# A decoder block on one core: the splits of the routing stage moved from GpSimd to VectorE, an f32 gate matrix, and a deeper run-ahead with activations in DRAM

## Chip, cores and metric

The kernel runs on one core of a Trainium2 chip. The metric is the device time of one execution, in microseconds.

## What is computed

One decoder block on 256 tokens of width 2048, all in float32: a mixer (retention and dilated attention), attention to 256 memory tokens, and the part that the change touches, a product-key expert layer. From the normed rows `hf` a query product gives scores against two sets of 128 keys per head (8 heads). Per token and head the best 16 of each set are taken, their 256 sums formed, the best 16 of these chosen, and a softmax over them gives 16 gates. Each choice names an expert (i1, i2) out of 128 × 128 = 16384. The result is

    a = gelu(hf @ u_tab[i].T);   y = sum over the 128 choices of (a * gate) * v_tab[i]

A last RMS norm follows.

## The kernel before

The expert layer is computed densely: all 16384 columns of the first table `u` are multiplied, in 32 chunks of 512, and all rows of the second table `v`; a gate matrix G (256 × 16384, mostly zeros) stands in for the choice. So the whole kernel is one stream of 464 weight pieces of 128 × 4 × 512 floats (1 MiB), and a piece is 24 TensorE matmuls of 512 columns: every f32 operand is split into two parts `hi` + `lo` (ScalarE writes `hi`, line 973; a subtraction writes `lo`, line 974), and three products make one exact product (lines 197 to 199).

*Order.* The program is written out by hand: each engine runs its instructions in the order in which the Python code emits them. `ahead` (line 966) emits the loads, on SP's queue, and the splits, two pieces ahead of the products (three raw buffers, so loads run about five pieces ahead). Between pieces `tick` (line 119) advances background generators. A generator that yields a cost may go on within a budget: 4.0 a tick, half of it when `fine` is set, and then there is a second tick in the middle of each piece. `fine` holds from the first piece of `u` until the gate matrix is done.

*Routing* (one generator, `route`): `route_top` (line 655, 32 steps of a top 16 over 128 keys), `route_pairs` (670, twice 8 heads of sums and a top 16 over 256, then one-hot selections of the key numbers, lines 701 to 704), `route_gates` (709: Exp on ScalarE, sums on VectorE, then on TensorE the transposes of line 726), and `gate_matrix` (741). All but these transposes, the Exp and some copies is VectorE's.

*Gate matrix.* In 32 steps of 8 tokens, VectorE builds, for each 4 tokens, bf16 one-hot rows for i2 (line 755) and i1 (756), and three products of the latter with the gate's three bf16 parts (758); TensorE sums 3 products per token (767, bf16, 128 columns); ScalarE copies them (768) and SP's queue writes 512 KB to G in DRAM (769). The matmuls of a step are emitted one step later than its one-hots.

*Tables.* 11 chunks of `u` (RUN_AHEAD) run before the first piece of `v`; their splits' `lo`, and those of the query product `w_pq`, are on GpSimd (`"pool"` in lines 935 and 942, taken up in 974). `evac_u` (777) writes a chunk's Gelu into an SBUF unit that is kept until `weigh` (787) loads the chunk's columns of G on SP's queue, multiplies (808) and transposes them (`to_T`, 168) for the second table. Then groups of 8 pieces of `v` alternate with 8 pieces of `u` until `u` is used up. The SBUF buffers called `unit` are a pool of 29.

Of the kernel before, what the change touches and what calls it, by code (L numbers as in the profile page):

```python
# [31 lines left out]
RUN_AHEAD = 11  # L32
# [3 lines left out]
TICK = 4.0  # L36

# [33 lines left out]
def block_kernel(ctx, tc, a, out):  # L71
# [47 lines left out]
    def tick():  # L119
        """One step of each; a step that yields a cost lets the next follow within the budget."""  # L120
        for g in list(active):
            spent, most = 0.0, TICK * (0.5 if fine[0] else 1.0)
            try:
                while spent < most:
                    spent += next(g) or TICK
            except StopIteration:
                active.remove(g)

    def add(g):
        active.append(g)  # L130
        return g
# [9 lines left out]
    def piece(ap, fn, lo_eng=None):  # L141
        prog.append((ap, fn, lo_eng))

    def call(fn):
        prog.append((None, fn, None))

# [54 lines left out]
    def chunks(wap, lhs, nk, order, evac, lo_eng=None):  # L201
        """Row products: for chunk n, k group kq in `order`, acc[n] += lhs[kq].T @ w piece."""
# [20 lines left out]
        for n, kq in order:  # L223
            c = seen.get(n, 0)
            seen[n] = c + 1
            piece(wap[n * nk + kq], make(n, kq, c == 0, c == nk - 1), lo_eng)
# [28 lines left out]
    def make_trig():  # L255
        """cos, sin, -sin of f32(position) * angle, its multiple of 2 pi taken off exactly."""
# [54 lines left out]
    def evac_rot(kind, key):  # L311
        """Rotated rows from [4 heads x first halves | 4 heads x second halves]."""
# [342 lines left out]
    def route_top(n):  # L655
        """The 16 best keys of each half query of chunk n, both token blocks."""
        while sc_rows[n] is None:
            yield
        for tb in range(2):
# [5 lines left out]
            for i in range(4):  # L665
                top16(rt[tb]["v"][:, 4 * n + i], rt[tb]["i"][:, 4 * n + i], sc_rows[n][:, tb, i], work([128]))
                yield 1.0
        sc_rows[n] = 0

    def route_pairs(tb):  # L670
        """Top 16 of the 256 sums per head, their experts' two key numbers and gates."""
# [10 lines left out]
        for h0 in range(0, 8, 4):  # L682
            combo = unit([4, 256])
            for h in range(h0, h0 + 4):
# [4 lines left out]
                yield 2.0  # L689
# [19 lines left out]
    def route_gates():  # L709
# [12 lines left out]
        for tb in range(2):  # L722
# [4 lines left out]
            rest = uc[:, 3]  # L727
            tt = uc[:, 4:6].rearrange("p a b -> p (a b)").bitcast(BF).rearrange("p (s t) -> p s t", t=128)
            i3 = uc[:, 0].bitcast(BF)[:, 0:128]
            nc.scalar.copy(rest, tp[:, 2])  # L730
            for s in range(2):
                nc.scalar.copy(tt[:, s], tp[:, s])
            nc.scalar.copy(tt[:, 2], rest)
            nc.vector.tensor_sub(rest, rest, tt[:, 2])
            nc.vector.tensor_copy(tt[:, 3], rest)
            nc.vector.tensor_sub(rest, rest, tt[:, 3])
            nc.vector.tensor_copy(i3, rest)
            rt[tb] = {"T": [tt[:, 0], tt[:, 1], tt[:, 2], tt[:, 3], i3]}
        yield

    def gate_matrix():
# [3 lines left out]
        iota4 = cp.tile([128, 128, 4], BF, name="iota4")  # L745
        nc.vector.tensor_copy(iota4, bc(iota[:, :, None], [128, 128, 4]))
        prev = None
        for tb, t0 in [(tb, t0) for tb in range(2) for t0 in range(0, 128, 8)] + [(None, None)]:
            cur = []
            if tb is not None:  # L750
                it = rt[tb]["T"]
                for t1 in (t0, t0 + 4):
                    oh = unit([4, 128, 4], BF)
                    col = [bc(z[:, None, t1:t1 + 4], [128, 128, 4]) for z in it]
                    nc.vector.tensor_tensor(oh[:, 0], iota4, col[1], op=OP.is_equal)  # L755
                    nc.vector.tensor_tensor(oh[:, 3], iota4, col[0], op=OP.is_equal)  # L756
                    for j in (1, 2, 3):
                        nc.vector.tensor_tensor(oh[:, j], oh[:, 3], col[1 + j], op=OP.mult)  # L758
                    cur.append(oh)
            if prev is not None:  # L760
                ptb, p0, ohs = prev
                gs = unit([8, 128])
                for j, oh in enumerate(ohs):
# [7 lines left out]
            yield  # L771
# [5 lines left out]
    def evac_u(c, acc):  # L777
# [3 lines left out]
        ga[c] = g  # L781
# [5 lines left out]
    def weigh():  # L787
        """Expert activations times gates, transposed for the second table's products."""
# [12 lines left out]
        for c in range(N_CH):  # L801
            while c not in ga or c > 2 * v_at[0] + 3:
# [4 lines left out]
            g, m = ga.pop(c), w.pop(c)  # L807
# [127 lines left out]
    chunks(a["w_pq"], hf_T, KQ, late, evac_rows_T(pq_T, "rstd2"), "pool")  # L935

    def u_chunk(c, eng=None):
        chunks(a["u"][c * KQ:c * KQ + KQ], hf_T, KQ, straight(0, 1), lambda _, acc: evac_u(c, acc), eng)

    call(lambda: fine.__setitem__(0, True))  # L940
    for c in range(RUN_AHEAD):
        u_chunk(c, "pool")
# [23 lines left out]
    def ahead(n):  # L966
        while at["split"] < min(n + SPLIT_AHEAD + 1, len(stream)):
# [33 lines left out]
    for ap, fn, _ in prog:  # L1001
# [29 lines left out]
def _pieces(w, cols=None):  # L1031
    """[K, N] -> [N/512 * K/512, 128, 4, 512]: blocks of 512 x 512, a k row per partition."""
# [66 lines left out]
```

## Time and profile before

| | us |
|---|---|
| median of 3 runs (lowest, highest) | 2840.21 (2840.13, 2842.31) |
| span of the profiled execution | 2843.3 |
| TensorE matmul busy | 2764.3 (97%) |
| VectorE busy | 1698.7 (60%) |
| ScalarE busy | 1160.1 (41%) |
| GpSimd busy | 378.0 (13%) |

The page gives the profiled execution's span, from the first to the last instruction, and no other time of its own. Matmuls overlap, so TensorE's busy share says only whether it had something to do; how fast it went is read from the spacing of starts. The page also cuts the span into 40 slices of 71 us, a digit for the tenths that an engine was busy.

### The profile page before, as it was taken

What the parts mean: (1) busy time and instruction counts of PE and PEld (TensorE: products, weight loads), DVE (VectorE), ACT (ScalarE), POOL (GpSimd) and SP (SyncE); (2) the same over time, 40 slices, a digit from 0 to 9 for tenths busy, and PEclk for the clock granted to TensorE, in tenths of its full rate; (3) what the DMA queues carried; (4) which work ended last, traced back from release to release, by engine and by line L of the source; (5) the groups of instructions that cost most, each with busy time, mean ns of one, the idle gap of its engine ahead of it and who ended that gap; (6) DMA issues with size and microseconds to landing.
All of it is one profiled execution on the core that took longest, in us unless ns stands there. A gap on an engine that the chain in (4) does not pass through costs nothing.

```text
span 2843.3 us, 31283 instructions
## 1 busy us (share of the span) xinstructions
PE 2764.3 (97%) x12898; PEld 2296.9 (81%) x12898; DVE 1698.7 (60%) x1872; ACT 1160.1 (41%) x1053; POOL 378.0 (13%) x153
## 2 busy tenths in 40 slices
PE   9999999999999999999299999999999999999998
PEld 7888888888888888888188788888888888888886
DVE  6565457785643445179999655455554555545664
ACT  6444334433554434444133334333343333433333
POOL 1111110011000000778133400000000000000001
PEclk9999999999999999999699999999999999999999
DMA  8554555576655445545156655555555555555653
GB/s 291 192 181 169 191 180 181 202 263 218 246 199 188 156 145 179 179 176 194 58 163 178 198 195 203 205 192 199 207 204 204 191 200 207 203 204 201 220 207 127
DMA packets 118736, 546.95 MB, mean 192 GB/s; under 512 B 10176, under 2 KB 42944, under 8 KB 59712
## 3 DMA queue, kind: packets, MB, share of 16 engines
q1 hardware_dynamic: 113488, 526.46, 53.3%
q0 software_dynamic: 5104, 18.48, 1.8%
q8 instruction: 101, 1.65, 0.2%
q14 instruction: 43, 0.35, 0.0%
HBM read 521.83 MB, written 23.07 MB: 192 GB/s over the span
## 4 chain that ended last, share of the span: by engine, by line
PE 84%; DVE 12%; issue 1%; POOL 1%; DMA 0%; ACT 0%; SPq 0%; POOLq 0%; DVEq 0%
PE acc L197 27%; PE acc L199 27%; PE acc L198 27%; DVE unit L758 3%; DVE unit L756 2%; PE tp L180 2%; DVE unit L703 1%; DVE unit L755 1%; DVE unit L685 1%; DVE unit L701 1%; POOL unit L327 1%; PE sm L610 0%; PE sm L579 0%; DVE unit L648 0%; DVE unit L645 0%
## 5 line engine op out<-in xcount | busy, mean ns | idle before, releaser
L197 PE MATMUL acc<-hi,unit 128*128 128x512 f32 x3712 | 1461.8, 394 | 6.9 <-ACT hi L993 6.9
L199 PE MATMUL acc<-hi,unit 128*128 128x512 f32 x3712 | 1448.1, 390 | 0.0
L198 PE MATMUL acc<-lo,unit 128*128 128x512 f32 x3712 | 1448.1, 390 | 0.0
L974 DVE TENSOR_TENSOR lo<-raw,hi 128x2048 fp32r<-128x2048 f32 (+1 forms) x404 | 922.9, 2285 | 833.2 <-ACT hi L973 829.7
L973 ACT CAST hi<-raw 128x2048 fp32r<-128x2048 f32 (+1 forms) x464 | 881.7, 1901 | 895.4 <-PE acc L199 776.0
L197 PEld LDWEIGHTS acc<-hi,unit 128*128 128x128 f32 x3712 | 699.8, 189 | 148.1 <-ACT hi L993 7.0
L199 PEld LDWEIGHTS acc<-hi,unit 128*128 128x128 f32 x3712 | 698.7, 188 | 146.4
L198 PEld LDWEIGHTS acc<-lo,unit 128*128 128x128 f32 x3712 | 699.5, 188 | 142.1 <-DVE lo L994 0.9
L974 POOL TENSOR_TENSOR lo<-raw,hi 128x2048 fp32r<-128x2048 f32 x60 | 278.6, 4645 | 549.7 <-ACT hi L973 549.7
L849 POOL DMA_DIRECT2D unit<-in_g_final_dram x2 | 1.1, 561 | 1052.3 <-ACT unit L185 1042.2
L767 PE MATMUL sm<-unit 128*128 128x128 bf16 x768 | 102.3, 296 | 9.9 <-DVE unit L758 9.8
L767 PEld LDWEIGHTS <-unit 128*128 128x128 bf16 x768 | 84.0, 117 | 27.5 <-DVE unit L758 22.3
L833 DVE TENSOR_TENSOR unit<-unit,acc 128x512 f32<-128x512 f32 x128 | 87.5, 687 | 27.1 <-PE acc L199 26.7
L185 ACT CAST unit<-tp 128x512 fp32r<-128x512 f32 x76 | 40.8, 589 | 152.6 <-PE tp L180 152.6
L758 DVE TENSOR_TENSOR unit<-unit 128x512 bf16<-128x512 bf16 x192 | 93.3, 513 | 4.4
L186 DVE TENSOR_TENSOR unit<-tp,unit 128x512 fp32r<-128x512 f32 x76 | 48.9, 684 | 75.8 <-ACT unit L185 75.8
L768 ACT COPY unit<-sm 128x512 f32<-128x512 f32 x64 | 37.5, 587 | 119.5 <-PE sm L767 108.6
L780 ACT ACTIVATE unit<-acc,rstd 128x512 f32<-128x512 f32 x64 | 43.6, 690 | 89.4 <-PE acc L199 79.3
L180 PE MATMUL tp<-ident,unit 128*128 128x128 f32 x544 | 71.9, 273 | 4.2 <-DVE unit L808 2.9
L180 PEld LDWEIGHTS tp<-ident,unit 128*128 128x128 f32 x544 | 63.1, 140 | 14.6 <-POOL unit L327 3.5
L756 DVE TENSOR_TENSOR unit<-iota,unit 128x512 bf16<-128x512 bf16 x64 | 70.8, 1106 | 0.0
L327 POOL TENSOR_TENSOR unit<-work 128x512 f32<-128x512 f32 x20 | 37.7, 1887 | 176.4 <-DVE work L325 175.2
(191 smaller groups left out, 920.0 us busy)
## 6 DMA issues: line engine op xcount, KB each, us to landing
raw<-in_u_dram SPq DMA_DIRECT2D x128, 1024.0 KB, 4.8
raw<-in_v_dram SPq DMA_DIRECT2D x128, 1024.0 KB, 4.7
raw<-in_w_in_dram SPq DMA_DIRECT2D x96, 1024.0 KB, 4.7
raw<-in_w_kv_dram SPq DMA_DIRECT2D x32, 1024.0 KB, 4.7
raw<-in_w_out_dram SPq DMA_DIRECT2D x16, 1024.0 KB, 4.8
raw<-in_w_qm_dram SPq DMA_DIRECT2D x16, 1024.0 KB, 4.9
raw<-in_w_om_dram SPq DMA_DIRECT2D x16, 1024.0 KB, 4.7
raw<-in_w_pq_dram SPq DMA_DIRECT2D x16, 1024.0 KB, 4.7
```

Source lines behind the costliest of these rows:

```text
L180: nc.tensor.transpose(tp[:, k, tb * 128:tb * 128 + 128], rows[:, tb, f:f + 128], ident)
L186: nc.vector.tensor_sub(lo[:, s], tp, hi[:, s])
L197: nc.tensor.matmul(acc, lh, rh, start=start, stop=False)
L198: nc.tensor.matmul(acc, lh, rl, start=False, stop=False)
L199: nc.tensor.matmul(acc, ll, rh, start=False, stop=stop)
L327: nc.gpsimd.tensor_add(rows[:, tb].rearrange("p (h two c) -> p two h c", h=4, two=2), A.rearrange("p (two h) c -> p two h c", two=2), B.re ...
L756: nc.vector.tensor_tensor(oh[:, 3], iota4, col[0], op=OP.is_equal)
L758: nc.vector.tensor_tensor(oh[:, j], oh[:, 3], col[1 + j], op=OP.mult)
L767: nc.tensor.matmul(p[:, i], oh[:, k, :, i], oh[:, 0, :, i], start=(k == 1), stop=(k == 3))
L833: nc.vector.tensor_add(r[:, tb], r[:, tb], acc[tb])
L973: nc.scalar.copy(hi[:, ks], raw[:, ks])
L974: (nc.gpsimd if stream[i][2] == "pool" else nc.vector).tensor_sub(lo[:, ks], raw[:, ks], hi[:, ks])
```

## The change

It puts all splits of the stream on VectorE; runs 20 chunks of the first table ahead instead of 11; writes each chunk's Gelu to DRAM on GpSimd's queue and reads it back, on SP's queue, beside the chunk's columns of G; builds the one-hots in f32, the gate already multiplied in, with one tensor_scalar per token and side; and sums them with one f32 matmul a token. `tick` now keeps a credit per generator (1.5 a tick in the fine stage, 4.0 otherwise; a step that overdraws it is paid back in later ticks), and the steps declare new costs.

```diff
-RUN_AHEAD = 11
+RUN_AHEAD = 20
+FINE = 1.5
...
     def tick():
+        gain = FINE if fine[0] else TICK
         for g in list(active):
-            spent, most = 0.0, TICK * (0.5 if fine[0] else 1.0)
+            credit[g] = min(credit[g], 0.0) + gain
             try:
-                while spent < most:
-                    spent += next(g) or TICK
+                while credit[g] > 0.0:
+                    credit[g] -= next(g) or gain
             except StopIteration:
                 active.remove(g)
...
                 top16(rt[tb]["v"][:, 4 * n + i], ...)
-                yield 1.0
+                yield 1.57
...
                 top16(cv[:, h], ci[:, h], combo[:, h - h0], work([256]))
-                yield 2.0
+                yield 2.75
...
                     if h == h0 + 2:
-                        yield 2.0
+                        yield 1.4
...
-            nc.scalar.copy(rest, tp[:, 2])
-            for s in range(2):
-                nc.scalar.copy(tt[:, s], tp[:, s])
-            nc.scalar.copy(tt[:, 2], rest)
-            nc.vector.tensor_sub(rest, rest, tt[:, 2])
-            nc.vector.tensor_copy(tt[:, 3], rest)
-            nc.vector.tensor_sub(rest, rest, tt[:, 3])
-            nc.vector.tensor_copy(i3, rest)
-            rt[tb] = {"T": [tt[:, 0], tt[:, 1], tt[:, 2], tt[:, 3], i3]}
+            tt = uc[:, 3:6]
+            nc.scalar.copy(tt, tp)
+            rt[tb] = {"T": tt}
...
     def gate_matrix():
...
-                for t1 in (t0, t0 + 4):
-                    oh = unit([4, 128, 4], BF)
-                    col = [bc(z[:, None, t1:t1 + 4], [128, 128, 4]) for z in it]
-                    nc.vector.tensor_tensor(oh[:, 0], iota4, col[1], op=OP.is_equal)
-                    nc.vector.tensor_tensor(oh[:, 3], iota4, col[0], op=OP.is_equal)
-                    for j in (1, 2, 3):
-                        nc.vector.tensor_tensor(oh[:, j], oh[:, 3], col[1 + j], op=OP.mult)
+                cur = unit([8, 128]), unit([8, 128])
+                for i in range(8):
+                    t = slice(t0 + i, t0 + i + 1)
+                    nc.vector.tensor_scalar(cur[0][:, i], iota, it[:, 0, t], it[:, 2, t],
+                                            op0=OP.is_equal, op1=OP.mult)
+                    nc.vector.tensor_scalar(cur[1][:, i], iota, it[:, 1, t], None, op0=OP.is_equal)
...
-                        for k in (1, 2, 3):
-                            nc.tensor.matmul(p[:, i], oh[:, k, :, i], oh[:, 0, :, i], start=(k == 1), stop=(k == 3))
+                        nc.tensor.matmul(p[:, i], lh[:, 4 * j + i], rh[:, 4 * j + i], start=True, stop=True)
...
-            yield
+            yield 2.6
...
     def evac_u(c, acc):
...
-        ga[c] = g
+        d = dp.tile([128, 2, 512], F32, name=f"act{c}")
+        nc.gpsimd.dma_start(d, g)
+        ga[c] = d
...
         def load(c):
-            w[c] = unit([2, 512])
+            w[c] = unit([2, 512]), unit([2, 512])
             for tb in range(2):
-                nc.sync.dma_start(w[c][:, tb], G_d[tb][:, c * 512:c * 512 + 512])
+                nc.sync.dma_start(w[c][0][:, tb], G_d[tb][:, c * 512:c * 512 + 512])
+            nc.sync.dma_start(w[c][1], ga.pop(c))
...
-            while c not in ga or c > 2 * v_at[0] + 3:
+            while (c + 1 < N_CH and c + 1 not in ga) or c > 2 * v_at[0] + 3:
...
-                (nc.gpsimd if stream[i][2] == "pool" else nc.vector).tensor_sub(lo[:, ks], raw[:, ks], hi[:, ks])
+                nc.vector.tensor_sub(lo[:, ks], raw[:, ks], hi[:, ks])
```

## Rows read from the trace of the kernel before

**Rows 1.** From the page: the span, each engine's busy time with its share and instructions, and three lines of the 40 slices (busy tenths of TensorE and VectorE; the granted clock of TensorE in tenths).
```profile
span 2843.3 us, 31283 instructions
...
PE 2764.3 (97%) x12898; PEld 2296.9 (81%) x12898; DVE 1698.7 (60%) x1872; ACT 1160.1 (41%) x1053; POOL 378.0 (13%) x153
...
PE   9999999999999999999299999999999999999998
...
DVE  6565457785643445179999655455554555545664
...
PEclk9999999999999999999699999999999999999999
```

**Rows 2.** The waits of TensorE over the whole span: tile and line that waited, what it waited for, us in total, times, longest us.
```profile
PE tp L726 <- DVE unit L720: 41.1, 1, 41.1
PE sm L767 <- DVE unit L758: 9.8, 23, 6.0
...
PE tp L726 <- DVE unit L704: 5.1, 1, 5.1
```

**Rows 3.** A table by stretch (us from the span's start): length, then busy us and instructions of TensorE, its weight loads, VectorE, ScalarE and GpSimd, the granted clock, the share of the DMA engines and GB/s.
```profile
1242.00:1350.00 108.00, 108.00 (x490) 89.81 (x489) 98.95 (x171) 47.15 (x34) 89.41 (x21) 1.00 0.53 186
1350.00:1417.00 67.00, 14.83 (x58) 11.25 (x56) 62.91 (x146) 8.26 (x15) 13.88 (x3) 0.62 0.15 51
1417.00:1606.00 189.00, 185.11 (x1139) 154.51 (x1140) 183.59 (x317) 70.66 (x87) 70.62 (x15) 0.97 0.59 171
...
1651.00:2600.00 949.00, 949.00 (x4276) 787.56 (x4275) 504.78 (x325) 374.17 (x256) 0.00 (x0) 1.00 0.57 201
```

**Rows 4.** ScalarE's timeline from 1255 to 1660, the Gelu at the end of a first-table chunk: start, us, engine, line, operation, what it writes and reads, count; in brackets the idle time before it and what ended it.
```profile
1287.41 1.37 ACT L780 ACTIVATE unit<-acc,rstd 128x512 f32<-128x512 f32 x2 [2.80 <-PE acc L199]
...
1309.17 1.37 ACT L780 ACTIVATE unit<-acc,rstd 128x512 f32<-128x512 f32 x2 [2.80 <-PE acc L199]
...
1330.93 1.37 ACT L780 ACTIVATE unit<-acc,rstd 128x512 f32<-128x512 f32 x2 [2.81 <-PE acc L199]
...
1650.29 1.37 ACT L780 ACTIVATE unit<-acc,rstd 128x512 f32<-128x512 f32 x2 [2.34 <-PE acc L199]
```

**Rows 5.** TensorE's timeline from 1355 to 1650, same columns: the routing transposes (L726) and the gate matrix's matmuls (L767), of which consecutive ones stand in one row.
```profile
1402.84 1.23 PE L726 MATMUL tp<-ident,unit 128*128 128x128 f32 x4 [41.09 <-DVE unit L720]
...
1416.99 0.30 PE L767 MATMUL sm<-unit 128*128 128x128 bf16 x1 [5.97 <-DVE unit L758]
...
1447.49 2.99 PE L767 MATMUL sm<-unit 128*128 128x128 bf16 x24
...
1453.05 2.99 PE L767 MATMUL sm<-unit 128*128 128x128 bf16 x24
...
1604.98 1.34 PE L767 MATMUL sm<-unit 128*128 128x128 bf16 x10 [0.17 <-DVE unit L758]
```

**Rows 6.** The timelines of VectorE and GpSimd around 1350, where the two overlap, and VectorE's from 1364 to 1392, where GpSimd is idle, same columns: the start of two sums-of-pairs steps (L685) and the end of two selections (L704).
```profile
1350.26 4.82 DVE L701 TENSOR_TENSOR unit<-unit,iota 128x256 f32<-128x256 f32 x1
1355.11 0.43 DVE L703 TENSOR_TENSOR unit<-unit 128x256 f32<-128x256 f32 x1
...
1349.97 4.83 POOL L974 TENSOR_TENSOR lo<-raw,hi 128x2048 fp32r<-128x2048 f32 x1 [0.70 <-ACT hi L973]
...
1364.31 0.41 DVE L685 TENSOR_TENSOR unit<-unit 128x256 f32<-128x256 f32 x1
...
1367.01 0.41 DVE L685 TENSOR_TENSOR unit<-unit 128x256 f32<-128x256 f32 x1
...
1387.32 1.22 DVE L704 TENSOR_REDUCE unit<-unit 128x64 f32<-128x1024 f32 x1
...
1391.75 1.22 DVE L704 TENSOR_REDUCE unit<-unit 128x64 f32<-128x1024 f32 x1
```

**Rows 7.** VectorE's timeline near the start of the kernel, same columns: a split on VectorE and the instruction behind it, then tensor_scalars of 128 columns with a per-partition scalar (L261, two in one row) and without (L298, L300).
```profile
29.16 2.29 DVE L974 TENSOR_TENSOR lo<-raw,hi 128x2048 fp32r<-128x2048 f32 x1 [0.16 <-ACT hi L973]
31.37 0.16 DVE L258 CAST pf<-pos_i 128x2 f32<-128x2 int32 x1
31.57 0.48 DVE L261 TENSOR_SCALAR work<-ang_c,pf 128x128 f32<-128x128 f32 x2
...
60.61 0.23 DVE L298 TENSOR_SCALAR trig<-unit 128x128 f32<-128x128 f32 x1
60.76 0.22 DVE L300 TENSOR_SCALAR trig<-trig 128x128 f32<-128x128 f32 x1
```

**Rows 8.** TensorE's timeline at a scoring product (L635, 16 f32 matmuls of 128 columns) and the next piece, same columns; then the group of the f32 matmuls of 256 columns (line, engine, operation, shapes, count, busy us, mean ns, idle before).
```profile
1248.02 1.95 PE L635 MATMUL sm<-unit 128*128 128x128 f32 x16
1249.72 0.48 PE L197 MATMUL acc<-hi,unit 128*128 128x512 f32 x1
1250.03 0.40 PE L198 MATMUL acc<-lo,unit 128*128 128x512 f32 x1
...
L579 PE MATMUL sm<-unit 128*128 128x256 f32 x64 | 14.5, 379 | 0.0
```

**Rows 9.** DMA issues: what is written from what, queue, operation, count, KB each, median us from issue to landing.
```profile
gate_r<-unit POOLq DMA_DIRECT2D x4, 512.0 KB, 3.6
...
unit<-gate_r POOLq DMA_DIRECT2D x4, 512.0 KB, 5.5
```

**Rows 10.** The waits of SP's queue, columns as in group 2.
```profile
SPq L769 <- ACT unit L768: 78.8, 17, 6.8
```

More of the change, by code (lines that the diff above doesn't have):

```diff
@@ L119, in tick @@
     def tick():
+        gain = FINE if fine[0] else TICK
         for g in list(active):
-            spent, most = 0.0, TICK * (0.5 if fine[0] else 1.0)
+            credit[g] = min(credit[g], 0.0) + gain
             try:
-                while spent < most:
-                    spent += next(g) or TICK
+                while credit[g] > 0.0:
+                    credit[g] -= next(g) or gain
             except StopIteration:
                 active.remove(g)
+    credit = {}
     def add(g):
         active.append(g)
+        credit[g] = 0.0
         return g
@@ L139, in block_kernel, with piece @@
     prog = []
-    def piece(ap, fn, lo_eng=None):
-        prog.append((ap, fn, lo_eng))
+    def piece(ap, fn):
+        prog.append((ap, fn))
     def call(fn):
-        prog.append((None, fn, None))
+        prog.append((None, fn))
     def rstd_of(ssq, n, shape, name):
@@ L199, in mm3, with chunks @@
         nc.tensor.matmul(acc, ll, rh, start=False, stop=stop)
-    def chunks(wap, lhs, nk, order, evac, lo_eng=None):
+    def chunks(wap, lhs, nk, order, evac):
         accs = {}
@@ L225, in chunks @@
             seen[n] = c + 1
-            piece(wap[n * nk + kq], make(n, kq, c == 0, c == nk - 1), lo_eng)
+            piece(wap[n * nk + kq], make(n, kq, c == 0, c == nk - 1))
     def straight(n0, n1, nk=KQ):
@@ L726, in route_gates @@
                 nc.tensor.transpose(tp[:, s], sel[:, s].rearrange("p h k -> p (h k)"), ident)
-            rest = uc[:, 3]
-            tt = uc[:, 4:6].rearrange("p a b -> p (a b)").bitcast(BF).rearrange("p (s t) -> p s t", t=128)
-            i3 = uc[:, 0].bitcast(BF)[:, 0:128]
-            nc.scalar.copy(rest, tp[:, 2])
-            for s in range(2):
-                nc.scalar.copy(tt[:, s], tp[:, s])
-            nc.scalar.copy(tt[:, 2], rest)
-            nc.vector.tensor_sub(rest, rest, tt[:, 2])
@@ L735, in route_gates @@
-            nc.vector.tensor_copy(tt[:, 3], rest)
-            nc.vector.tensor_sub(rest, rest, tt[:, 3])
-            nc.vector.tensor_copy(i3, rest)
-            rt[tb] = {"T": [tt[:, 0], tt[:, 1], tt[:, 2], tt[:, 3], i3]}
+            tt = uc[:, 3:6]
+            nc.scalar.copy(tt, tp)
+            rt[tb] = {"T": tt}
         yield
     def gate_matrix():
-        iota4 = cp.tile([128, 128, 4], BF, name="iota4")
-        nc.vector.tensor_copy(iota4, bc(iota[:, :, None], [128, 128, 4]))
         prev = None
@@ L748, in gate_matrix @@
         for tb, t0 in [(tb, t0) for tb in range(2) for t0 in range(0, 128, 8)] + [(None, None)]:
[L749 removed]
+            cur = None
             if tb is not None:
                 it = rt[tb]["T"]
[L752 to L759 removed]
+                cur = unit([8, 128]), unit([8, 128])
[4 more added lines that the diff above has]
+                    nc.vector.tensor_scalar(cur[1][:, i], iota, it[:, 1, t], None, op0=OP.is_equal)
@@ L760, in gate_matrix @@
             if prev is not None:
-                ptb, p0, ohs = prev
+                ptb, p0, (lh, rh) = prev
                 gs = unit([8, 128])
-                for j, oh in enumerate(ohs):
+                for j in range(2):
                     p = bank("sm", [4, 128])
                     for i in range(4):
-                        for k in (1, 2, 3):
-                            nc.tensor.matmul(p[:, i], oh[:, k, :, i], oh[:, 0, :, i], start=(k == 1), stop=(k == 3))
+                        nc.tensor.matmul(p[:, i], lh[:, 4 * j + i], rh[:, 4 * j + i], start=True, stop=True)
@@ L806, in weigh @@
             yield
-            g, m = ga.pop(c), w.pop(c)
+            m, g = w.pop(c)
             nc.vector.tensor_mul(g, g, m)
@@ L934, in block_kernel, with u_chunk @@
     call(lambda: add(weigh()))
-    chunks(a["w_pq"], hf_T, KQ, late, evac_rows_T(pq_T, "rstd2"), "pool")
-    def u_chunk(c, eng=None):
-        chunks(a["u"][c * KQ:c * KQ + KQ], hf_T, KQ, straight(0, 1), lambda _, acc: evac_u(c, acc), eng)
+    chunks(a["w_pq"], hf_T, KQ, late, evac_rows_T(pq_T, "rstd2"))
+    def u_chunk(c):
+        chunks(a["u"][c * KQ:c * KQ + KQ], hf_T, KQ, straight(0, 1), lambda _, acc: evac_u(c, acc))
     call(lambda: fine.__setitem__(0, True))
     for c in range(RUN_AHEAD):
-        u_chunk(c, "pool")
+        u_chunk(c)
     for gi in range(N_CH // 2):
@@ L1000, in block_kernel @@
     n = 0
-    for ap, fn, _ in prog:
+    for ap, fn in prog:
         if ap is None:
```

## The prediction, on record before the changed kernel was run

> **What bounds the kernel now.** I read the page first. TensorE is at 9 tenths in every slice but the 20th and the last, VectorE is nearly full in slices 19 to 22, and the granted clock leaves 9 only in slice 20 [rows 1]. So this is a TensorE-bound kernel with one wound, and the question is how long the wound is. The waits of TensorE name it: 41.1 and 5.1 us, both before the three-plane transposes of line 726, which sit in TensorE's queue between pieces of the first expert table and wait for VectorE's routing; all other waits are about 10 us [rows 2]. The table by stretch places it: TensorE stands from 1356 to 1403 while VectorE is full, and afterwards, to 1606, both look full [rows 3].
>
> How much is lost is read from the ends of the first-table chunks, which ScalarE marks with its Gelu. Undisturbed, a chunk of four pieces takes 21.76 us (1287.41, 1309.17, 1330.93), 5.44 a piece. The chunk whose Gelu starts at 1287.41 and the last chunk ahead, 1650.29, are nine chunks apart: 362.9 us instead of 9 × 21.76 = 195.8 [rows 4]. **167.0 us** in this stretch are not table products. After 1651 TensorE is full and the clock whole [rows 3], so nothing is to be had there.
>
> Of the 167.0, the gate matrix is the largest part. It goes from 1416.99 to 1604.98 + 1.34, that is 189 us, with a half piece between two steps of eight tokens. A step with 24 bf16 matmuls and its half piece repeats every 5.56 us, of which the half piece is 2.72: 2.84 us for 24 matmuls, 0.118 each [rows 5]. The rest is the 46.2 us of waiting, 6.0 more ahead of the first step [rows 5], and the slow matmuls after the stop.
>
> Why VectorE is late is seen in two timelines laid side by side: GpSimd's split runs from 1349.97 for 4.83 us, and the VectorE instruction that starts at 1350.26 ends with it, 4.82 us long, where its neighbours take 0.42 [rows 6]. Each split on GpSimd thus holds VectorE for about 4.4 us a piece; the same split on VectorE occupies it 2.21 us (29.16 to 31.37) [rows 7].
>
> **The change part by part.**
>
> *Splits to VectorE.* Sixty splits leave GpSimd's queue and join VectorE's. Beside the routing, VectorE then has 2.21 us of split a piece and, by the new budget, two ticks of 1.5 of background steps. Are those costs true? One sums-of-pairs step declares 2.75 and repeats every 2.70; the four heads of a one-hot selection declare 4.0 and repeat every 4.43 [rows 6]. So VectorE needs 5.2 to 5.5 us against 5.44 of TensorE: just enough, and the few pieces at 5.5 lag by under 2 us, less than the two pieces by which splits run ahead. What ends the 46.2 us is this: VectorE no longer falls behind the place where line 726 stands in TensorE's queue. There stays a hand-over (Exp, sums, transposes); I take 3 us, between 0 and the 5.1 of the shorter wait [rows 2].
>
> *One f32 matmul a token.* 768 bf16 matmuls go, 256 f32 ones of the same 128 columns come. The nearest row is the f32 scoring product: 16 start at 1248.02 and the next piece at 1249.72, with 0.09 more lost at its first matmul, so 0.106 each and 0.09 for the change over: 0.94 a step of eight, **30 us** for 32 steps [rows 8]. Lower end: no change-over, 27. Upper end: the f32 matmul of 256 columns, 14.5/64 = 0.227 each, 58 us [rows 8].
> The Trainium skill (FP8 and Floating Point Precision, section TensorE Precision Notes) says that true FP32 takes four passes through the array. By that rule, and taking the 0.227 us of a 512-column f32r matmul as one pass, 256 matmuls would cost 58 us, and the total would be 28 us more; the row of the scoring product speaks against it.
>
> *One-hots.* Per eight tokens ten bf16 instructions go and sixteen f32 tensor_scalars of 128 columns come, eight with two per-partition scalars, eight with one. The trace has one such with one scalar: two in a row take 0.48 us, the second about 0.28, so 0.20 from start to start; without a per-partition scalar two starts are 0.15 apart [rows 7]. I take 0.20: 3.2 us a step. Counting the ticks, 33 gate steps run over 28 pieces, so a step has 0.875 piece: TensorE 0.875 × 5.44 + 0.94 = 5.70 us, VectorE 0.875 × 2.21 + 3.2 = 5.13. TensorE is the bound as long as a one-hot costs under 0.236. Lower end 0.15, which gains nothing; upper end the whole duration plus 0.06 for a second scalar, 0.28 and 0.34: 5.0 a step, 6.9 against 5.70, 39 us.
> Steps fall two ticks apart, but 8 of 32 only one, and 4 of these within a piece. There TensorE asks for a step's one-hots 2.7 us after they were issued, behind a split; about 1.2 us each, **5 us**, between 0 and 4 × 2.7 = 11.
>
> *Twenty chunks ahead.* By the count of ticks the gate matrix ends at the 62nd of 80 pieces and the first weighted chunk is transposed at the 66th: 14 pieces, 76 us, to spare. Pieces and transposes are only put in another order, at no cost while TensorE is full.
>
> *Activations in DRAM.* 32 writes on GpSimd's queue, behind which stand only later writes and the last norm's gain; 32 reads on SP's queue, behind which stand the table's loads. A read waits for a write that is far older (the first two at the 64th piece, written by the 8th), so SP isn't held; the loads are five pieces ahead and can give the 5.5 us of such a read [rows 9]. I cost them at nothing; the cover is DMA time. It is thinnest in the gate stretch: loads alone take 0.53 of the engines at 186 GB/s [rows 3]; the gate stretch before loads 15.5 pieces in 189 us, 86 GB/s or 0.245, so of its 0.59 the gate matrix has 0.345, 2.04 us a step. After: 0.875 piece of loads 2.52, gate matrix 2.04, activations 0.32, together 4.9 of 5.70 us. It fits. Uncovered, all 33.5 MB at 186/0.53 = 351 GB/s would be 96 us.
> The gate matrix's write still waits on SP for ScalarE's copy (78.8 us in all before [rows 10]); now 0.875 of a piece lies between two steps instead of a half, so no load behind it is later than before.
>
> **Sum.** of the 167.0, 22 transposes of 128 columns stay (six of line 726, sixteen of the weighing), at 0.106 each 2.3; 164.7 goes; − 30 f32 matmuls − 5 adjacent steps − 3 hand-over = **126.7 us** gained. Span 2843.3 − 126.7 = 2716.6. The page gives the span alone, 3.1 above the median of the runs, 2840.21 [rows 1]; so **2714 us**.
>
> **The rivals.**
>
> *VectorE becomes the bound of the gate stretch.* For it: 5.13 of 5.70 us is 90% of it, and no row shows a tensor_scalar with two per-partition scalars. Against: the 0.20 was measured next to other work. At 0.284 to 0.34 each it costs 25 to 39 us: 2739 to 2753. Chance 0.17.
>
> *An f32 matmul costs double the scoring row*, 0.227 instead of 0.106: 28 us more, 2742. Against it stand the scoring matmuls, of exactly this shape. Chance 0.05.
> This is where the four-pass rule of the Trainium skill (the section named above) would put it; the trace, at 0.106, does not agree with it so far.
>
> *The DRAM round trip takes the place of the stall: slower.* An activation write is late, the read of it on SP waits, and every table load behind stands still. The gate arrays made the trip at 3.6 us out and 5.5 back [rows 9]; if all of it were exposed for 32 chunks, 291 us: 3005. It is slower from 126.7/32 = 4.0 us exposed a chunk. For it: SP's queue is in order. Against: 18 chunks lie between write and read. Chance 0.05.
> The Trainium skill (SBUF — State Buffer, section Who interferes with whom) says that a VectorE instruction in a two-port mode, which an f32 tensor_scalar may take, keeps GpSimd from writing the descriptors of its DMAs; that would delay these writes. No run here shows it yet; it holds only if a delay reaches 18 chunks.
>
> *The change doesn't do what it says*: VectorE lags more than the 76 us of reserve, and the stop merely moves to the start of the second table. It would need VectorE at over 6.4 us a piece through 80 pieces; the gain shrinks to nothing, about 2840. Chance 0.03.
>
> **How the numbers follow.** Forecast 0.70, the rivals 0.17, 0.05, 0.05, 0.03. The low end is the sum with no new wait and the cheapest matmuls, 2714 − 11 = 2703, with a little for waits that I left standing: 2700. The high end takes in the first two rivals: 2755. A measurement can tell 0.2%, 5.7 us, from no change. Faster 0.93 (0.70 + 0.17 + 0.05 and a third of the last), same 0.02, slower 0.05.
>
> **What would show it.** Right: no wait at the routing transposes over 5 us; Gelu starts 21.8 us apart until the gate stretch and about 26 in it; VectorE instructions of 0.42 nowhere at 4.8; splits 2.3 us throughout; a whole clock. Wrong: TensorE waiting for one-hots at each step (first rival), f32 matmuls more than 0.11 apart (second), SP waiting at the activation reads with TensorE idle after 1700 (third), a stop at the first piece of the second table (fourth).

## The result, and the profile after

The changed kernel takes **2737.4 us** (median of 4 runs, 2736.5 to 2738.0) against 2841.3 for the kernel before, run beside it (4 runs, 2840.1 to 2844.5): a ratio of 0.9632, 95% interval 0.9618 to 0.9646. It is faster, as forecast, and lies inside the range of 2700 to 2755, but 23 us above the forecast of 2714.

The page of the changed kernel: span, busy times, and two of its slice lines, VectorE's and the granted clock, to be laid beside [rows 1].

```profile
span 2734.7 us, 31099 instructions
...
PE 2715.8 (99%) x12642; PEld 2266.7 (83%) x12642; DVE 1691.2 (62%) x2115; ACT 1160.0 (42%) x1047; POOL 116.4 (4%) x125
...
DVE  7566447886554444569998885445555455666664
...
PEclk9999999999999999999999999999999999999999
```

The wound is closed: the granted clock is whole in every slice. VectorE still has three slices at nine tenths, but TensorE no longer waits for it there. The span is 108.6 us shorter. GpSimd lost 262 us of its busy time. VectorE took over sixty splits, 137 us at 2.29 each, and is yet busy 7.5 us *less* than before. In the run below that moves the splits and nothing else it is busy 1697.1 us: the splits only replace time for which VectorE had been held.

All waits of TensorE (what waited, for what, us in total, times, longest us), beside [rows 2]:

```profile
PE acc L202 <- ACT hi L987: 6.3, 1, 6.3
PE tp L185 <- POOL unit L332: 1.4, 6, 0.2
```

Of the 41.1, 9.8 and 5.1 us of [rows 2] nothing is left. What remains stands in the first 400 us of the kernel, and was there before (6.9 and 1.4).

The table by stretch (columns as in [rows 3]): routing, gate matrix, and two stretches behind it.

```profile
1241.00:1419.00 178.00, 178.00 (x799) 147.82 (x798) 168.78 (x370) 75.92 (x55) 4.14 (x8) 1.00 0.60 210
...
1428.00:1592.00 164.00, 164.00 (x927) 143.22 (x926) 140.92 (x424) 78.10 (x83) 2.69 (x5) 1.00 0.76 234
1592.00:1680.00 88.00, 88.00 (x455) 75.10 (x454) 60.40 (x130) 40.72 (x40) 2.14 (x4) 1.00 0.82 273
```

In the routing VectorE is busy 168.8 of 178 us and TensorE does not wait for it; in the gate stretch VectorE has 23 us to spare. So the gate stretch is now TensorE's, and its length is TensorE's own work. The ends of the first-table chunks (ScalarE's timeline, the Gelu, as [rows 4]) show how much that is:

```profile
1286.41 1.37 ACT L771 ACTIVATE unit<-acc,rstd 128x512 f32<-128x512 f32 x2 [2.85 <-PE acc L204]
...
1416.97 1.37 ACT L771 ACTIVATE unit<-acc,rstd 128x512 f32<-128x512 f32 x2 [2.84 <-PE acc L204]
...
1441.22 1.37 ACT L771 ACTIVATE unit<-acc,rstd 128x512 f32<-128x512 f32 x2 [1.08 <-PE acc L204]
1471.98 1.37 ACT L771 ACTIVATE unit<-acc,rstd 128x512 f32<-128x512 f32 x2 [1.47 <-PE acc L204]
1502.74 1.37 ACT L771 ACTIVATE unit<-acc,rstd 128x512 f32<-128x512 f32 x2 [1.47 <-PE acc L204]
1531.70 1.37 ACT L771 ACTIVATE unit<-acc,rstd 128x512 f32<-128x512 f32 x2 [2.39 <-PE acc L204]
...
1739.99 1.37 ACT L771 ACTIVATE unit<-acc,rstd 128x512 f32<-128x512 f32 x2 [2.85 <-PE acc L204]
```

Chunks are 21.76 us apart through the whole routing (1286.41 to 1416.97 is 6 × 21.76), where the kernel before stopped. In the gate stretch they are 30.76 or 28.96 apart: five or four steps of 1.8 us on top of 21.76. The forecast had about 26 there. From 1286.41 to 1739.99 there are 18 chunks, 391.7 us of table products, and 61.9 us of other work.

What a step costs is in TensorE's timeline: the routing transposes, which wait for nothing, then one step of eight tokens and the table piece behind it.

```profile
1425.62 0.82 PE L731 MATMUL tp<-ident,unit 128*128 128x128 f32 x6
...
1453.46 1.95 PE L758 MATMUL sm<-unit 128*128 128x128 f32 x16
1455.16 0.48 PE L202 MATMUL acc<-hi,unit 128*128 128x512 f32 x1
1455.48 0.40 PE L203 MATMUL acc<-lo,unit 128*128 128x512 f32 x1
```

The code issues **eight** f32 matmuls a step; the row holds **sixteen** records. They take 1.70 us to the start of the next piece and its first matmul another 0.09 (1455.16 to 1455.48 is 0.32 instead of 0.23): 1.79 a step, 57.3 for 32. With 4.0 us for 38 transposes at 0.106 (six of line 731, and 32 of the weighing, eight of line 185 for each of four chunks) that leaves 0.6 of the 61.9.

Groups by line (count, busy us, mean ns), and VectorE's timeline in the gate stretch:

```profile
L758 PE MATMUL sm<-unit 128*128 128x128 f32 x512 | 62.2, 275 | 0.0
L640 PE MATMUL sm<-unit 128*128 128x128 f32 x64 | 7.8, 275 | 0.0
```

```profile
1438.87 2.29 DVE L968 TENSOR_TENSOR lo<-raw,hi 128x2048 fp32r<-128x2048 f32 x1 [1.75 <-ACT hi L967]
1441.08 0.34 DVE L749 TENSOR_SCALAR unit<-iota,unit 128x128 f32<-128x128 f32 x1
1441.34 0.28 DVE L751 TENSOR_SCALAR unit<-iota,unit 128x128 f32<-128x128 f32 x1
1441.54 0.34 DVE L749 TENSOR_SCALAR unit<-iota,unit 128x128 f32<-128x128 f32 x1
```

512 records stand for 256 matmuls. The scoring product (line 640, line 635 before) is the same: 64 records, and its loops issue 4 × 2 × 4 = 32. The one-hot with two per-partition scalars takes 0.26 from start to start (1441.08 to 1441.34), the one with one scalar 0.20; 16 of them 3.63 (1441.08 to 1444.51 + 0.20). Splits take 2.29.

The DMA issues of the round trip, and SP's wait at the write of G:

```profile
act<-unit POOLq DMA_DIRECT2D x32, 512.0 KB, 4.4
unit<-act SPq DMA_DIRECT2D x32, 512.0 KB, 6.4
```

```profile
SPq L760 <- ACT unit L759: 53.2, 25, 4.1
```

A write lands 4.4 us after its issue, a read 6.4, a little more than the gate arrays of [rows 9], and SP waits less for the copies of the gate matrix than before [rows 10].

### The profile page after: what moved, and what is told of

It reads as the page before. It is cut to its first block, busy times and chain, and to the rows that moved or that the text cites. A ratio compares the mean times of both kernels' runs of the same rounds, so it can differ in the third digit from the quotient of the medians.

```text
span 2734.7 us, 31099 instructions
## 1 busy us (share of the span) xinstructions
PE 2715.8 (99%) x12642; PEld 2266.7 (83%) x12642; DVE 1691.2 (62%) x2115; ACT 1160.0 (42%) x1047; POOL 116.4 (4%) x125
## 4 chain that ended last, share of the span: by engine, by line
PE 98%; POOL 1%; DVE 1%; issue 0%; DMA 0%; POOLq 0%; SPq 0%; ACT 0%; DVEq 0%
PE acc L202 30%; PE acc L204 30%; PE acc L203 30%; PE tp L185 2%; PE sm L758 2%; POOL unit L332 1%; PE sm L584 1%; PE sm L615 1%; PE sm L456 0%; PE sm L478 0%; DVE work L326 0%; PE sm L640 0%; DVE work L330 0%; DMA raw<-in_w_in_dram 0%; PE tp L472 0%
## 5 line engine op out<-in xcount | busy, mean ns | idle before, releaser
L968 DVE TENSOR_TENSOR lo<-raw,hi 128x2048 fp32r<-128x2048 f32 (+1 forms) x464 | 1060.1, 2286 | 822.7 <-ACT hi L967 819.0
L749 DVE TENSOR_SCALAR unit<-iota,unit 128x128 f32<-128x128 f32 x256 | 88.4, 345 | 0.0
L751 DVE TENSOR_SCALAR unit<-iota,unit 128x128 f32<-128x128 f32 x256 | 73.0, 285 | 0.0
L773 POOL DMA_DIRECT2D act<-unit x32 | 17.1, 535 | 1109.0 <-ACT unit L771 1109.0
L758 PEld LDWEIGHTS sm<-unit 128*128 128x128 f32 x512 | 62.0, 191 | 2.5
L758 PE MATMUL sm<-unit 128*128 128x128 f32 x512 | 62.2, 275 | 0.0
L389 DVE RECIPROCAL unit<-unit 128x256 f32<-128x256 f32 x32 | 56.1, 1754 | 1.1
L188 ACT COPY unit<-tp 128x512 f32<-128x512 f32 x44 | 23.7, 592 | 59.2 <-PE tp L185 59.2
```

What stands on the lines that cost most here:

```text
L389: nc.vector.reciprocal(rows[:, tb, c], rows[:, tb, c])
L749: nc.vector.tensor_scalar(cur[0][:, i], iota, it[:, 0, t], it[:, 2, t], op0=OP.is_equal, op1=OP.mult)
L751: nc.vector.tensor_scalar(cur[1][:, i], iota, it[:, 1, t], None, op0=OP.is_equal)
L758: nc.tensor.matmul(p[:, i], lh[:, 4 * j + i], rh[:, 4 * j + i], start=True, stop=True)
L968: nc.vector.tensor_sub(lo[:, ks], raw[:, ks], hi[:, ks])
```

## The experiments

Two questions were open: why the gate matrix's matmuls cost twice the forecast, and which part of the change ended the stop. A last group tests the depth and the round trip. All times are medians; the changed kernel's is 2737.4. An interval is that of the ratio to the kernel before.

### The price of a gate matmul

**Each f32 matmul issued twice** (the second does the first one's work again).

```diff
                     for i in range(4):
                         nc.tensor.matmul(p[:, i], lh[:, 4 * j + i], rh[:, 4 * j + i], start=True, stop=True)
+                        nc.tensor.matmul(p[:, i], lh[:, 4 * j + i], rh[:, 4 * j + i], start=True, stop=True)
```

> Each f32 matmul of the gate matrix is issued twice (the second overwrites the first). Theory: the term of the sum that failed is the f32 matmul; in the changed kernel's trace one f32 matmul is two TensorE instructions, 1.70 us for eight tokens, and TensorE is the bound throughout, so doubling them costs 32 x 1.70 = 54 us: 2737 + 54 = 2792. Rival, the price of the prediction (0.106 a matmul, 0.85 a step): 27 us, 2765. If VectorE were the bound of the gate stretch: under 10 us.

Measured 2795.6 (0.9836, 0.982 to 0.9852): 58.2 us for 256 matmuls more, 0.227 each. The group of the first of the two lines; the second has as many records:

```profile
L758 PE MATMUL sm<-unit 128*128 128x128 f32 x512 | 98.8, 275 | 0.0
```

TensorE got no new wait by it. An f32 matmul of 128 columns costs two records of about 0.11 us each, on the path. Both rivals fall: the price of the prediction (27 us) and VectorE as the bound (under 10).

**One-hots as fp32r**, one fp32r matmul a token; this leaves out the low bits of the gates.

```diff
-                cur = unit([8, 128]), unit([8, 128])
+                cur = unit([8, 128], F32R), unit([8, 128], F32R)
```

> The one-hots are written as fp32r, so that each token takes one fp32r matmul; the low bits of the gates are left out. Theory: one TensorE instruction instead of two a token. At the spacing of the f32 instruction (0.106) it saves 32 x 0.85 = 27 us, at a quarter of the 512-column fp32r one (0.057) 40 us; from there VectorE, 5.56 us a step, is the bound at 0.2 to 0.6 a step more, which gives 8 to 15 back: 2703 to 2712. Rival (something else than the matmuls made up the missing 19 us): 2730 to 2737.

Measured 2715.2 (0.9554, 0.9538 to 0.957), 22.2 us less than the changed kernel: 3 us above the theory's range, and below the rival's. The group, and two steps in TensorE's timeline:

```profile
L758 PE MATMUL sm<-unit 128*128 128x128 f32 x256 | 35.4, 271 | 1.6 <-DVE unit L751 0.4
```

```profile
1468.85 1.60 PE L758 MATMUL sm<-unit 128*128 128x128 f32 x7
1470.64 0.33 PE L758 MATMUL sm<-unit 128*128 128x128 f32 x1 [0.20 <-DVE unit L751]
1470.81 0.45 PE L202 MATMUL acc<-hi,unit 128*128 128x512 f32 x1
...
1476.32 1.00 PE L758 MATMUL sm<-unit 128*128 128x128 f32 x8
1477.17 0.45 PE L202 MATMUL acc<-hi,unit 128*128 128x512 f32 x1
```

One record a matmul now, eight in 0.85 and a step in 0.95 (the step after 1452.39 starts at 1458.78, a piece of 5.44 between): the 0.94 of the forecast, with half the instructions, and of the theory's two prices the higher one, 0.106. 32 × (1.79 − 0.95) is 26.9 us; 22.2 were measured. The rest is the row at 1468.85: this step comes only half a piece after the one before, and its matmuls follow VectorE's one-hots one by one, 1.96 us until the next piece instead of 0.85. Four steps of this stretch are drawn out like that (at 1468.85, 1509.24, 1555.98 and 1598.50), to 1.96, 1.90, 2.46 and 1.89: 4.8 us together, the forecast's term for adjacent steps (four at 1.2). 26.9 − 4.8 = 22.1. Hardly any of it shows as a wait (0.4 us).

**The gate split in two fp32r parts**: two fp32r matmuls a token and eight more one-hots a step (the step declares 5.2, with 25 chunks ahead).

```diff
-                cur = unit([8, 128]), unit([8, 128])
+                cur = unit([8, 128], F32R), unit([8, 128], F32R), unit([8, 128], F32R)
...
-                        nc.tensor.matmul(p[:, i], lh[:, 4 * j + i], rh[:, 4 * j + i], start=True, stop=True)
+                        nc.tensor.matmul(p[:, i], lh[:, 4 * j + i], rh[:, 4 * j + i], start=True, stop=False)
+                        nc.tensor.matmul(p[:, i], ll[:, 4 * j + i], rh[:, 4 * j + i], start=False, stop=True)
```

> A candidate: the gate is split into two fp32r parts, so that two fp32r matmuls a token sum to the f32 product; three tensor_scalars a token (5.7 us a step), a step declared at 5.2, and 25 chunks ahead to make room. TensorE issues 512 instructions as in the changed kernel. If an fp32r one of 128 columns takes 0.057: 25 us less, 2712. If it takes 0.106 like the f32 one: no change, 2737. If VectorE doesn't keep up: slower.

Measured 2739.2 (0.964, 0.9623 to 0.9656), 1.8 us above the changed kernel: not 0.057 each. In TensorE's timeline the starts are 0.11 apart:

```profile
1473.79 0.27 PE L763 MATMUL sm<-unit 128*128 128x128 f32 x1
1473.90 0.27 PE L764 MATMUL sm<-unit 128*128 128x128 f32 x1
```

So two fp32r matmuls cost what one f32 matmul costs. At this size a cheaper type saved nothing here; fewer instructions did.

**The bf16 gate matrix of before** put back into the changed kernel (three bf16 parts, 768 matmuls; the new tick and everything else kept).

```diff
-                cur = unit([8, 128]), unit([8, 128])
+                for t1 in (t0, t0 + 4):
+                    oh = unit([4, 128, 4], BF)
...
-                        nc.tensor.matmul(p[:, i], lh[:, 4 * j + i], rh[:, 4 * j + i], start=True, stop=True)
+                        for k in (1, 2, 3):
+                            nc.tensor.matmul(p[:, i], oh[:, k, :, i], oh[:, 0, :, i], start=(k == 1), stop=(k == 3))
```

> The changed kernel with the gate matrix of the kernel before (bf16 one-hots, three bf16 matmuls a token). Theory: 2.84 us a step instead of 1.79, TensorE the bound: 32 x 1.05 = 34 us slower, 2771. By the price of the prediction (0.94 a step): 61 us, 2798. If the gate matrix were hidden: 2737.

Measured 2771.2 (0.9754, 0.9738 to 0.9771), 33.8 above: the f32 gate matrix is worth 34 us of the gain. By instructions: 768 at the 0.118 of [rows 5] are 91 us, 512 at 0.106 with the change-over 57, 256 about 30. The first difference, 34, is the 33.8 of this run; the second, 27, is the 22.2 of the fp32r kernel and the 4.8 of its adjacent steps.

### What ended the stop

**Splits back on GpSimd**, those of `w_pq` and of the first 20 chunks, the rest of the change kept.

```diff
-                nc.vector.tensor_sub(lo[:, ks], raw[:, ks], hi[:, ks])
+                (nc.gpsimd if 192 <= i < 288 else nc.vector).tensor_sub(lo[:, ks], raw[:, ks], hi[:, ks])
```

> The changed kernel with the splits of the query product and of the first 20 chunks back on GpSimd. Theory (a split there holds VectorE's two-input instructions): VectorE loses about 4.4 us a piece against 2.2 for the split itself while sums of pairs and selections run (25 pieces), some 50 us of lag, and again while one-hots are built if they are held too: TensorE stands at the routing transposes, 2790 to 2815. Rival (20 chunks of run-ahead absorb it): 2737 to 2745.

Measured 2790.0 (0.9819, 0.9802 to 0.9835): 52.6 more, the low end of the theory. These are 96 splits on GpSimd, 36 more than in the kernel before, and twenty of the 36 run before the last one-hots are built, so 52.6 us is not the price of the sixty. Waits of TensorE, 35.5 us of it, then VectorE's timeline at two splits, then GpSimd's:

```profile
PE tp L731 <- DVE unit L725: 18.3, 1, 18.3
PE sm L758 <- DVE unit L751: 17.2, 16, 3.1
```

```profile
1481.11 4.72 DVE L749 TENSOR_SCALAR unit<-iota,unit 128x128 f32<-128x128 f32 x1
...
1488.48 4.66 DVE L751 TENSOR_SCALAR unit<-iota,unit 128x128 f32<-128x128 f32 x1
```

```profile
1481.16 4.59 POOL L968 TENSOR_TENSOR lo<-raw,hi 128x2048 fp32r<-128x2048 f32 x1 [5.67 <-ACT hi L967]
1488.40 4.65 POOL L968 TENSOR_TENSOR lo<-raw,hi 128x2048 fp32r<-128x2048 f32 x1 [2.65 <-ACT hi L967]
```

At both splits the VectorE instruction in hand ends within 0.1 us of the split's end (1485.75 and 1493.05): the mechanism of [rows 6], now on the one-hots, both forms. The groups of the routing, with GpSimd's splits beside them:

```profile
L708 DVE TENSOR_TENSOR unit<-unit 128x256 f32<-128x256 f32 x19 | 42.6, 2243 | 0.7
L690 DVE TENSOR_TENSOR unit<-unit 128x256 f32<-128x256 f32 x14 | 40.4, 2887 | 0.0
...
L652 DVE MAX8 unit<-work 128x8 f32<-128x256 f32 x15 | 6.4, 428 | 0.5
...
L651 DVE MATCH_REPLACE8 work<-unit 128x256 f32<-128x256 f32 x15 | 6.1, 410 | 0.0
```

The second of these groups in the changed kernel:

```profile
L690 DVE TENSOR_TENSOR unit<-unit 128x256 f32<-128x256 f32 x16 | 6.7, 418 | 0.0
```

These two tensor_tensors take 2.2 to 2.9 us in the mean (0.42 without GpSimd's splits, in the changed kernel), MAX8 its usual 0.43, MATCH_REPLACE8 0.41 and FIND_INDEX8 0.42: not every VectorE operation is held. The Trainium skill (SBUF — State Buffer, section Who interferes with whom) lists tensor_tensor with two SBUF inputs, and tensor_scalar where it takes both ports, as contending with GpSimd; the 4.72 us one-hot beside the 4.59 us split agrees.

**The old budget**: the tick of before together with the costs that its steps declared; everything else as in the changed kernel. The lines below are those of the tick.

```diff
-            credit[g] = min(credit[g], 0.0) + gain
+            spent, most = 0.0, TICK * (0.5 if fine[0] else 1.0)
...
-                while credit[g] > 0.0:
-                    credit[g] -= next(g) or gain
+                while spent < most:
+                    spent += next(g) or TICK
...
```

> The changed kernel with the old tick budget and the old declared costs. Theory (the new budget removed the stop): VectorE falls behind again, TensorE stands 30 us at the routing transposes, 2767 to 2775. Rival (moving the splits removed it): 2737 to 2742.

Measured 2779.3 (0.9781, 0.9765 to 0.9798): 41.9 more, 4 above the theory's range. TensorE's waits:

```profile
PE acc L202 <- DVE lo L967: 21.9, 17, 2.4
...
PE tp L730 <- DVE unit L724: 3.0, 1, 3.0
```

The lag has changed its face. The routing transposes hardly wait, where the theory had 30 us; the *splits* come late, as they now stand on VectorE behind more routing steps than a piece has room for. Two of the 2.70 us steps and a split are 7.6 us against the piece's 5.44. These waits are 24.9 of the 41.9 us. About 7 more stand in no wait: the old budget issues eight gate steps a chunk, its Gelu starts are 37.7 to 38.7 us apart there, and TensorE's own work is 21.76 + 8 × 1.79 = 36.1. The other 10 were not placed; the granted clock, 0.96 from 1241 to 1425, has a part in them.

**Only the splits on VectorE**, the kernel before otherwise.

```diff
-                (nc.gpsimd if stream[i][2] == "pool" else nc.vector).tensor_sub(lo[:, ks], raw[:, ks], hi[:, ks])
+                nc.vector.tensor_sub(lo[:, ks], raw[:, ks], hi[:, ks])
```

> The kernel before with nothing changed but the splits, all on VectorE. Theory of the prediction (the splits on GpSimd cause the stop of 46 us): the stop shrinks to under 5 us and the gate stretch to 5.56 us a step, 57 us faster, 2784. Rival (the old budget issues routing faster than it can run: 101 us of routing and 46 us of splits on VectorE against 114 us of pieces): the stop is still 32 us, and with 11 us from the gate stretch it is 25 us faster, 2816.

Measured 2808.8 (0.9885, 0.9868 to 0.9901), 32 us faster than before: not the 57 of the theory, and nearer the 25 of the rival, which had the place wrong. Its largest wait is that of the old budget, by line 198 here, and the 41.1 us stop, which the rival left at 32, is 3.2:

```profile
PE acc L198 <- DVE lo L974: 21.9, 17, 2.4
...
PE tp L726 <- DVE unit L720: 3.2, 2, 3.0
```

So the theory with which I went in, that GpSimd's splits alone caused the stop's cost, falls. Without them a part of the cost comes back as late splits; the new budget is what takes it out. The runs make a chain: the splits alone give 31.9 us, the f32 gate matrix, the depth and the round trip on top of them 29.5 (2808.8 to 2779.3), the new budget the last 41.9.

**Both old**: old budget and GpSimd's splits in the changed kernel, whose f32 gate matrix, DRAM round trip and 20 chunks stay. The edit is that of the old budget and that of GpSimd's splits, both shown above.

> The changed kernel with the old budget and the splits on GpSimd, f32 gate matrix and depth kept. Alone the old budget cost 42 us and the splits on GpSimd 53. If each loads VectorE by itself: the sum, 2832. If both only use the same reserve and lag: the larger of the two, 2790 to 2800.

Measured 2832.2 (0.9971, 0.9958 to 0.9984). By the numbers the two costs add: 41.9 + 52.6 = 94.5, and 94.8 were measured. The losses stand in other places, though: here the 36 further splits on GpSimd start after 1627, when the last gate matmul (1594) is done, and the waits are not those of either run. That the sum comes out this closely may be chance. The stop is back, within 0.1 us, in spite of the f32 gate matrix:

```profile
PE tp L730 <- DVE unit L724: 41.2, 1, 41.2
PE sm L757 <- DVE unit L750: 22.0, 7, 3.7
```

It leaves 8.5 us of gain for the rest of the change. So most of the 34 us that the f32 gate matrix is worth in the changed kernel seem to be hidden here, where TensorE waits 22.0 us for the one-hots (9.8 before). No run takes the f32 gate matrix alone out of this kernel, so this is not shown; it would mean that the worth of a cheaper matmul depends on which engine is late.

### Depth and the round trip

**11 and 17 chunks ahead** in the changed kernel.

```diff
-RUN_AHEAD = 20
+RUN_AHEAD = 11
```

> The changed kernel with 11 chunks ahead. By the count of ticks 12 of 32 gate steps are done when the 44 pieces end; the other 20 run with no pieces beside them, 20 x 3.63 = 73 us of VectorE against 36 us of TensorE, and the read of G, the product and the transpose lie open, about 20 us: 57 us slower, 2795. Rival (the routing is early enough anyway, the depth is worth nothing): 2737.

Measured 2794.1 (0.9835, 0.9818 to 0.9851): 56.7 more, as expected. TensorE's timeline of 11 ahead tells why:

```profile
1503.88 1.95 PE L758 MATMUL sm<-unit 128*128 128x128 f32 x16
...
1509.48 72.34 PE L758 MATMUL sm<-unit 128*128 128x128 f32 x320 [3.65 <-DVE unit L751]
...
1591.70 1.97 PE L185 MATMUL tp<-ident,unit 128*128 128x128 f32 x8 [9.88 <-DVE unit L802]
```

The first piece of `v` comes due with 20 gate steps still to do. They run with no table piece between them, at VectorE's 3.62 us a step (eight tokens, whose one-hots start 0.45 us apart in its timeline) instead of TensorE's 1.79: 36.5 us lost. With 3.65 at its start, 9.88 at its end and 3.3 at the next pieces that is 53 of the 57. Most of this loss shows in no wait: TensorE seems busy for 72 us while its 320 records stand 0.23 apart in the mean, not 0.106.

With `RUN_AHEAD = 17`:

> The changed kernel with 17 chunks ahead, 68 pieces. By the count of ticks the first weighted chunk is transposed at the 66th piece: no change, 2737. Rival (the count leaves out waits, and the 14 pieces of reserve are used): each piece short costs 5.4 us, up to 2760.

Measured 2737.5 (0.9633, 0.962 to 0.9646): the same as 20. The reserve is at least 3 chunks, 65 us; 76 were forecast.

**The round trip doubled**: each chunk's activations are also written to a second DRAM buffer and read back into a spare unit, 33.5 MB more.

```diff
+        d2 = dp.tile([128, 2, 512], F32, name=f"acu{c}")
+        nc.gpsimd.dma_start(d2, g)
...
+            nc.sync.dma_start(unit([2, 512]), d2)
```

> The changed kernel with each chunk's activations written twice and read twice (the second copy isn't used): 33.5 MB more. Theory (the DRAM round trip is covered by DMA time to spare): within 0.2%, 2732 to 2743. Rival (the DMA engines, at a share of 0.82 where gate matrix, loads and reads meet, are nearly the bound): 10 to 96 us slower, 2747 to 2833.

Measured 2740.3 (0.9643, 0.9629 to 0.9656): 2.9 us more, 0.1%; this interval and that of the changed kernel overlap. Its table by stretch:

```profile
1428.00:1592.00 164.00, 164.00 (x924) 143.09 (x923) 140.93 (x423) 77.67 (x83) 5.31 (x10) 1.00 0.82 257
1592.00:1680.00 88.00, 86.61 (x452) 73.83 (x451) 59.18 (x132) 40.90 (x41) 4.23 (x8) 1.00 0.85 290
```

The DMA engines have room even for this, 0.82 and 0.85 busy; the one new wait is 1.4 us in the second stretch. So the second trip costs at most about 3 us. No run takes the first one out; as nothing in TensorE's waits stems from it, it should cost no more.

## Why the prediction was right, and where not

**The bound and the wound: right.** TensorE-bound, one wound from 1350 on, its whole size read from the chunk ends. All 41.1 + 5.1 + 9.8 us of waits went, and the clock is whole. That 2737.4 lies within the range is partly luck: the upper end was drawn for the first two rivals, and two errors of the sum, 27.3 and 8 us, offset each other.

**The failed step: "One f32 matmul a token".** The term said that the sixteen records of [rows 8] are sixteen matmuls, "so 0.106 each … 0.94 a step of eight, 30 us". They are the records of eight. A step costs what the whole row of the scoring product cost, 1.70 + 0.09 = 1.79, and 32 steps 57.3 us: 27.3 us too little in the sum. The row was there, and right; what was missing was the count of matmuls that its source line issues, next to its xcount. The other row of [rows 8] was misread the same way: line 579 issues 32 matmuls for its 64 records, so one of 256 columns takes 0.45 us, and the upper end of the term, 0.227, had a right figure from a wrong reading. The second rival had the price (0.227 forecast for it, 0.213 in the trace, 0.227 by the doubled matmul) and nearly the time, 2742, with a chance of 0.05, since I held the same misread row against it. By the rule of the Trainium skill (FP8 and Floating Point Precision, section TensorE Precision Notes), four passes for a true FP32 product, with 0.227 us for a pass of 512 columns, an f32 matmul of 128 columns is estimated at 0.227. The price of the trace's two records of 0.106 agrees with that after all. It does not show the passes, as one fp32r matmul of this size costs 0.106 alone.

**The two wait terms: 8 us too much.** Neither the adjacent steps (5) nor the hand-over (3) cost anything: TensorE has no wait for line 751 or 725, and its steps stand in one row of sixteen. The adjacent steps were right for the matmul that was forecast: with one of 0.106 a token they are there, four times. A step of 1.79 gives VectorE the time that 0.94 did not, so the error in the first term took this one away.

**The sum.** 126.7 − 27.3 + 8 = 107.4 us, against 108.6 in the spans; about 1.0 of the rest stands before the stretch (the Gelu at 1286.41 was at 1287.41). The forecast also took 3.1 us off to go from the span to the median; the changed kernel's median is 2.7 *above* its span, so that correction went the wrong way and makes the rest of the 23 us: 18.1 by spans, 5.3 by this. The runs show why: each one's time is about 2 us above its own span (2736.5 against 2734.7 for the profiled one), so the profiled execution of the kernel before, with a span of 2843.3, took about 2845, some 4 us more than the median. The spans differ by 108.6 us, the medians by 103.9, so 4 to 5 us of the gain in spans belong to that one execution.

**Splits: right price, half the cause.** A split on GpSimd does hold VectorE (4.72 us beside 4.59), on VectorE it takes 2.29. But the prediction explained VectorE's lateness by this alone and took the budget as no more than a check on room. In the changed kernel, the runs put 53 us to splits on GpSimd (96 of them) and 42 to the budget.

**One-hots.** 0.20 was taken; measured 0.26 with two scalars, 0.20 with one, 0.227 in the mean, under the bound of 0.236. VectorE needs 5.56 us a step against TensorE's 0.875 × 5.44 + 1.79 = 6.55. The first rival did not come (its 39 us belong to 0.28 and 0.34, 0.31 in the mean; at 0.34 each its sum gives 54). With the cheap matmul it is 5.56 against 5.70, and the fp32r kernel, drawn out only where two steps come close, shows that this holds too.

**Twenty ahead, and DRAM at nothing: right.** 17 are as good, 11 cost 57 us; the trip doubled costs at most 3. The slower rival needed 4.0 us exposed a chunk, and TensorE has no wait for an activation. The writes' 4.4 us to land are far from 18 chunks of delay. The forecast's 4.9 us of DMA time a step are 0.75 of the measured step of 6.55; the gate stretch has 0.76.

Of the signs that were named, these came: no wait at the routing transposes, 21.76 us a chunk in the routing, splits at 2.3, no 0.42 us instruction at 4.8, a whole clock. Two came out against it: f32 matmuls more than 0.11 apart (0.213 as matmuls, though their records are 0.106 apart), and Gelu starts in the gate stretch 28.96 or 30.76 apart instead of about 26.

## What to carry to other kernels

Before a price per instruction is read from a row, divide its time by the operations that the *source line* issues, not by the records. A slot that an engine cannot fill in time shows up at whatever stands behind it: with splits on GpSimd it was a 41 us stop at the transposes, with splits on VectorE it was 22 us in 17 late splits, and only the new budget on top of the moved splits removed both (its credit and its declared costs were not tried apart). And a run-ahead depth belongs to the budget that goes with it: the new budget was worth 42 us with 20 chunks ahead, and with 11 the same kernel took 57 us more.

## What the runs showed of the hardware

- An f32 matmul stands in the trace as two MATMUL records (512 for 256), each 0.106 us at 128 columns, and 0.227 at 256 (line 579: 64 records for 32 matmuls, 14.5 us). An f32 transpose is one record (six for the six of line 731).
- 128-column matmuls, each with weights of its own, cost nearly the same a record in all types: 0.118 bf16, 0.106 to 0.111 fp32r, 0.106 for half of an f32 one, although 512 columns of fp32r take 0.227. What bounds them at this pace no run shows.
- A two-input tensor_tensor on GpSimd holds VectorE's two-input tensor_tensors and f32 tensor_scalars to its own end (up to 4.8 us), and leaves MAX8, FIND_INDEX8 and MATCH_REPLACE8 alone (0.43, 0.42 and 0.41 us).
- The 16 DMA engines ran at 0.85 busy and 290 GB/s for 88 us with 1.4 us of new waits on TensorE.
